# A decoder layer with an RWKV-7 branch: TensorE's order in the recurrence written out, and one chain step for two heads

## The chip, the cores and the metric

The kernel runs on one core of a Trainium2 chip. The metric is device time in microseconds (us) of one execution. The core has TensorE (PE, matrix products; PEld is its load of weights), VectorE (DVE), ScalarE (ACT), GpSimd (POOL) and SyncE (SP, which here issues every DMA). Each engine works through a queue of its own in order; semaphores tie the queues together.

## The reference

One layer over 1024 tokens of width 1024. After a norm, one product with `w_in` gives everything that the two branches of the mixer need. Branch A is a dilated window attention. Branch B is RWKV-7: for each of 16 heads of width 64 a state is carried through all tokens.

```
proj = h @ w_in[l]
S_t = S_{t-1} diag(w_t) + (S_{t-1} a_t) b_t^T + v_t k_t^T ;  y_t = S_t r_t
y  = (y - mean) * rsqrt(var + GN_EPS) * gn_w + gn_b + (sum(r*k*r_k)) * v
o_rwkv = y * (sigmoid(dg) @ g2)
merged = sigmoid(g_attn) * (o_attn @ wb[:256]) + sigmoid(g_rwkv) * (o_rwkv @ wb[256:])
x = x + gt1 * rms_norm(merged @ w_out)
x = x + gt2 * rms_norm(square(relu(norm(x) @ w_ff1)) @ w_ff2)
```

## The kernel before

Three stages follow one another: the start and the attention (to about 420 us of the span), the recurrence with branch B (to about 1364 us), then the merge, the output product and the feed-forward. Only the recurrence is touched by the change.

Channels go two heads at a time: a pair is 128 channels, one partition each, and there are eight pairs, m = 0 to 7. Time is cut into 16 chunks of 64 tokens. For each pair these steps follow one another; the letter is the one in the table `ORDER` (line 19).

- P, `pair_project`: three dense products with `w_in` (r, k, v). A dense job is 128 output channels by 1024 tokens: 8 blocks of k, each with a high and a low part of the float32 operands, 48 products of 128x512 in all (line 307). Its weights come by DMA in four pieces, are split by ACT (`w_h`) and POOL (`w_l`), and its result leaves one of two PSUM buffers `d` through ACT and DVE (`shifted`).
- E, `pair_lora`: small products for decay and rate, then tanh on ACT and a running sum on DVE. F, `pair_features`: the norm of k (`bones`, Ln, Exp), and the factors `ar` and `bk`.
- g, `pair_gram`: 32 small products, masked by DVE into `lm` and `fe`. V, `pair_values`. I, `pair_inverse`: a triangular inverse on DVE, 30 steps of two operations with a transpose before and behind (`lt`, lines 769 to 781).
- L, `pair_local`: `place` copies the inverse into block-diagonal tiles `bd`; three rounds of products (`s<-lt,bd`, line 838) give `eh`, and 32 products (`s<-fe,b`, line 853) the step matrices `fe`.
- C, `pair_chain`: the serial part. For each of 16 chunks and each of the two heads, one product of `fe` with the state `sv` (line 874); DVE scales the new state out of PSUM (line 877), and that is the operand of the head's next product.
- N, `pair_norm`: the norm of y, a transpose back, and the gate. G is one gate job: a dense job like those of P, whose result goes to DRAM for the merge. There are 16; the first runs ahead of the recurrence.

`ORDER` is the order in which the program issues these steps. It is not the order of the engines: a scheduler sorts the instructions by priority and by a cost model of its own, and puts dense products on TensorE where that model has TensorE waiting. Small products use two PSUM buffers `s`; those of E and of the norm of k use the buffers `d` of the dense jobs.

## Time and profile before

| | |
|---|---|
| median of 3 runs | 2263.57 us (2256.59 to 2266.53) |
| the profiled execution | 2252.45 us; its span, first to last instruction, 2250.7 us |
| TensorE busy | 2083.3 us (93% of the span), granted clock 0.968 of full |
| DVE, ACT, POOL busy | 1559.3, 1035.0, 602.6 us |
| recurrence, first to last product of the chains | 560.23 to 1310.86 us |

The granted clock is the share of 2.4 GHz that the chip gave TensorE; it has two levels, 1.2 and 2.4 GHz, so a mean of 0.968 is a mix. Busy shares over the whole span say little here, since the recurrence has other limits than the dense stages.

### The profile page before, as it was taken

What the parts mean: (1) busy time and instruction counts of PE and PEld (TensorE: products, weight loads), DVE (VectorE), ACT (ScalarE), POOL (GpSimd) and SP (SyncE); (2) the same over time, 40 slices, a digit from 0 to 9 for tenths busy, and PEclk for the clock granted to TensorE, in tenths of its full rate; (3) what the DMA queues carried; (4) which work ended last, traced back from release to release, by engine and by line L of the source; (5) the groups of instructions that cost most, each with busy time, mean ns of one, the idle gap of its engine ahead of it and who ended that gap; (6) DMA issues with size and microseconds to landing.
All of it is one profiled execution on the core that took longest, in us unless ns stands there. A gap on an engine that the chain in (4) does not pass through costs nothing. (4 is left out here: it accounts for less than half of the span.)

```text
span 2250.7 us, 28246 instructions
## 1 busy us (share of the span) xinstructions
PE 2083.3 (93%) x10002; PEld 1621.9 (72%) x10002; DVE 1559.3 (69%) x2857; ACT 1035.0 (46%) x2018; POOL 602.6 (27%) x455
## 2 busy tenths in 40 slices
PE   6899999988999989898989999999889999999997
PEld 2676766666777767676767778877667777788886
DVE  5845555458989787878777743436876553799988
ACT  4634533445454636454554442225744443533342
POOL 2504310321313131222122122201100000788850
PEclk9999999999999999999998999999999999999999
DMA  7513311110111110101011154432544333433232
GB/s 248 181 34 99 99 40 29 59 31 22 30 33 35 31 37 27 35 29 37 24 37 34 52 179 159 128 120 84 166 156 163 113 107 111 166 130 128 88 109 75
DMA packets 156315, 194.88 MB, mean 87 GB/s; under 512 B 10729, under 2 KB 110211, under 8 KB 154127
## 3 DMA queue, kind: packets, MB, share of 16 engines
q1 hardware_dynamic: 156175, 193.08, 25.8%
q8 instruction: 79, 1.29, 0.2%
q14 instruction: 61, 0.50, 0.1%
HBM read 152.14 MB, written 40.90 MB: 86 GB/s over the span
## 5 line engine op out<-in xcount | busy, mean ns | idle before, releaser
L307 PE MATMUL d<-hh,w_h 128*128 128x512 f32 x960 | 328.2, 414 | 8.0 <-ACT w_h L64 4.6
L307 PE MATMUL d<-hl,w_h 128*128 128x512 f32 x960 | 329.5, 413 | 2.9 <-DVE hl L280 2.9
L307 PE MATMUL d<-hh,w_l 128*128 128x512 f32 x960 | 324.2, 410 | 1.4 <-DVE w_l L65 1.3
L65 POOL TENSOR_TENSOR w_l<-w_t,w_h 128x256 fp32r<-128x256 f32 x160 | 128.3, 803 | 634.0 <-ACT w_h L64 288.7
L1108 PE MATMUL m<-op 128*128 128x512 f32 x1272 | 292.0, 391 | 6.3 <-DVE big L1344 2.4
L1108 PE MATMUL m<-big,op 128*128 128x512 f32 x1152 | 276.6, 401 | 8.0 <-ACT op L64 4.1
L1108 PEld LDWEIGHTS m<-op 128*128 128x128 f32 x1272 | 239.5, 189 | 58.5 <-POOL op L65 3.4
L1108 PEld LDWEIGHTS m<-big,op 128*128 128x128 f32 x1152 | 213.9, 189 | 70.8 <-DVE u L1219 5.3
L64 ACT CAST w_h<-w_t 128x256 fp32r<-128x256 f32 x272 | 108.4, 404 | 310.3 <-PE d L307 222.7
L307 PEld LDWEIGHTS d<-hh,w_h 128*128 128x128 f32 x960 | 180.4, 192 | 47.8 <-ACT w_h L64 5.8
L307 PEld LDWEIGHTS d<-hl,w_h 128*128 128x128 f32 x960 | 181.0, 192 | 44.9 <-issue 9.4
L307 PEld LDWEIGHTS d<-hh,w_l 128*128 128x128 f32 x960 | 180.1, 191 | 42.5 <-issue 7.9
L64 ACT CAST op<-t 128x512 fp32r<-128x512 f32 (+1 forms) x152 | 113.5, 775 | 174.5 <-PE m L1108 119.3
L153 POOL TENSOR_TENSOR macc<-macc,ada_t 128x512 f32<-128x512 f32 x56 | 87.2, 1559 | 179.5 <-ACT macc L151 160.7
L65 DVE TENSOR_TENSOR op<-t,op 128x512 fp32r<-128x512 f32 (+1 forms) x125 | 117.7, 962 | 20.5 <-ACT op L64 20.3
L1281 DVE TENSOR_TENSOR big<-big,m 128x1024 f32<-128x1024 f32 x88 | 104.7, 1210 | 11.9 <-PE m L1108 11.8
L1299 POOL TENSOR_TENSOR t<-big 128x1024 f32<-128x1024 f32 x7 | 23.1, 3303 | 325.8 <-DMA big<-in_w_ff_dram 325.4
L775 DVE TENSOR_TENSOR lt<-lt 64x30 f32<-64x30 f32 (+14 forms) x240 | 97.1, 404 | 8.2
L777 DVE TENSOR_TENSOR lt<-lt 64x30 f32<-64x30 f32 (+14 forms) x240 | 93.9, 391 | 7.7
L874 PEld LDWEIGHTS ch<-sv,fe 128*128 128x128 f32 x512 | 83.0, 190 | 20.2 <-DVE sv L877 8.9
L65 POOL TENSOR_TENSOR op<-t,op 128x1024 fp32r<-128x1024 f32 x27 | 88.4, 3275 | 7.1 <-ACT op L64 7.1
L65 DVE TENSOR_TENSOR w_l<-w_t,w_h 128x256 fp32r<-128x256 f32 x112 | 60.1, 545 | 40.3 <-ACT w_h L64 28.9
(381 smaller groups left out, 3888.4 us busy)
## 6 DMA issues: line engine op xcount, KB each, us to landing
w_t<-in_w_in_dram SPq DMA_DIRECT2D x240, 128.0 KB
ada_t<-in_ada_w_dram SPq DMA_DIRECT2D x64, 256.0 KB
fS<-ft SPq DMA_DIRECT2D x64, 256.0 KB
t<-in_w_ff_dram SPq DMA_DIRECT2D x16, 1024.0 KB
big<-fS SPq DMA_DIRECT2D x16, 1024.0 KB
big<-in_w_ff_dram SPq DMA_DIRECT2D x16, 1024.0 KB
x<-in_x_dram SPq DMA_DIRECT2D x16, 512.0 KB
ada_t<-in_ada_w_dram SPq DMA_DIRECT2D x16, 512.0 KB
```

The lines of the kernel that those rows point to most:

```text
L64: nc.scalar.copy(hi, t)
L65: (eng or nc.vector).tensor_tensor(lo, t, hi.bitcast(F32), OP.subtract)
L153: nc.gpsimd.tensor_tensor(acc, acc, t, OP.add)
L307: nc.tensor.matmul(p[:, 512 * half + cs.start:512 * half + cs.stop], a, b[half][k][:, cs], start=k == ks[0] and i == 0, stop=k == ks[-1] a ...
L775: nc.vector.tensor_tensor(q, lb[:, s + 1:32, s:s + 1].to_broadcast([64, n, s]), lb[:, s:s + 1, 0:s].to_broadcast([64, n, s]), OP.mult)
L777: nc.vector.tensor_tensor(lb[:, s + 1:32, 0:s], lb[:, s + 1:32, 0:s], q, OP.add)
L874: nc.tensor.matmul(ps[h][:, c8, :], fe[b][:, h, c8, :], sv[h][b][:, c8, :], start=True, stop=True)
L1108: self.nc.tensor.matmul(p, s, m, start=start and k == 0 and i == 0, stop=k == len(a) - 1 and i == 2, skip_group_check=not start)
L1281: nc.vector.tensor_tensor(acc[nm][h], acc[nm][h], ps2[h], OP.add)
L1299: vb.tensor_tensor(t3, wr[:, k2, h2], wr[:, k1, h2], OP.subtract)
```

## The change

`ORDER` goes. A method `recurrence` issues the steps; while `pinned` is set, TensorE's instructions keep exactly the order in which they are issued (`mm` and `tr`). From pair 1 on, the dense work (rows r, k, v of pairs 2 to 7 and gates 1 to 15, 33 jobs in all) is one stream, and `fill(us)` issues so much of it, in pieces of two products counted as 0.45 us. The amounts are the constants `FE` to `FN`. `fill_until` issues dense pieces until the v of the next pair is done. Gates 1 to 11 are spread over the pairs, and 12 to 15 come last; before, most gates stood behind the last chain.

The chain takes both heads in a step: two products into one PSUM tile, and one DVE operation that scales both states by a factor broadcast along 64 columns; `sv` holds both heads. E and the norm of k use PSUM buffers `s` in place of `d`. `pair_local` becomes `pair_moves` (up to the transposes) and `pair_solve`; `pair_norm` is cut into `pair_spread` and `pair_norm`. Tiles `lt` go from 3 to 6, and the weights of E get a buffer of their own.

```diff
-ORDER = "P0 E0 F0 g0 V0 I0 P1 L0 C0 E1 F1 N0 g1 I1 V1 L1 P2 G1 C1 E2 F2 N1 g2 I2 V2 L2 P3 G2 C2 E3 F3 N2 g3 I3 V3 L3 P4 G3 C3 E4 F4 N3 g4 I4 V4 L4 P5 G4 C4 E5 F5 N4 g5 I5 V5 L5 P6 G5 C5 E6 F6 N5 g6 I6 V6 L6 P7 G6 C6 E7 F7 N6 g7 I7 V7 L7 C7 N7 G7 G8 G9 G10 G11 G12 G13 G14 G15"
+LEAD, BETWEEN, LAST = (1, 2), ((3,), (4, 5), (6,), (7, 8), (9,), (10, 11)), (12, 13, 14, 15)
+FE, FF, FG, FI, FL, FM, FC, FN = 0.9, 6.0, 0.9, 22.0, 0.45, 0.45, 0.45, 9.0
...
-NBD, NFT, NLT, NW, NGT, NRK = 5, 6, 3, 4, 2, 4
+NBD, NFT, NLT, NW, NGT, NRK = 5, 6, 6, 4, 2, 4
...
+            self.recurrence(st, wp, psD, gS)
+    def recurrence(self, st, wp, psD, gS):
+        prs = {}
+        jobs = []
+        for j in LEAD:
+            jobs.append(("G", j))
+        for m in range(2, 8):
+            jobs += [(nm, m) for nm in "rkv"] + [("G", j) for j in BETWEEN[m - 2]]
+        jobs += [("G", j) for j in LAST]
+        self.fill_jobs, self.fill_done, self.fill_w, self.credit = jobs, set(), {}, 0.0
+        self.fill_at = self.fill_stream(st, wp, psD, gS, prs)
+        prs[0] = self.pair_project(st, 0)
+        self.pair_lora(st, prs[0], 0)
+        self.pair_norms(st, prs[0], 0)
+        self.pair_features(st, prs[0], 0)
+        self.pair_gram(st, prs[0], 0)
+        self.pair_values(st, prs[0], 0)
+        self.pair_inverse(st, prs[0], 0)
+        self.pair_moves(st, prs[0], 0)
+        prs[1] = self.pair_project(st, 1)
+        self.pair_solve(st, prs[0], 0)
+        self.pinned = True
+        for m in range(8):
+            pr, nx = prs[m], None
+            if m < 7:
+                if m:
+                    self.fill_until(("v", m + 1))
+                nx = prs[m + 1]
+                self.pair_lora(st, nx, m + 1)
+                self.fill(FE)
+                self.pair_norms(st, nx, m + 1)
+            self.pair_chain(st, pr, m)
+            if nx:
+                self.pair_features(st, nx, m + 1)
+                self.pair_spread(st, pr, m)
+                self.fill(FF)
+                self.pair_gram(st, nx, m + 1)
+                self.pair_inverse(st, nx, m + 1)
+                self.pair_values(st, nx, m + 1)
+                self.pair_norm(st, pr, m)
+                self.pair_moves(st, nx, m + 1)
+                self.fill(FI)
+                self.pair_solve(st, nx, m + 1)
+            else:
+                self.pair_spread(st, pr, m)
+                self.fill(FN)
+                self.pair_norm(st, pr, m)
+                self.fill_until(jobs[-1])
+        self.pinned = False
+    def mm(self, *a, **k):
+        i = self.nc.tensor.matmul(*a, **k)
+        return self.tc.keep_in_program_order(i) if self.pinned else i
+    def tr(self, *a, **k):
+        i = self.nc.tensor.transpose(*a, **k)
+        return self.tc.keep_in_program_order(i) if self.pinned else i
+    def fill_weights(self, wp, n):
+        if n < len(self.fill_jobs):
+            nm, i = self.fill_jobs[n]
+            c0 = C_GATE + 128 * i if nm == "G" else C_RWKV + 1024 * "rkv".index(nm) + 128 * i
+            self.fill_w[n] = self.load_w(wp, self.w("w_in")[:, c0:c0 + 128], "w", 2, NW, 2, self.nc.gpsimd)
+    def fill_stream(self, st, wp, psD, gS, prs):
+        self.fill_weights(wp, 0)
+        for n, (nm, i) in enumerate(self.fill_jobs):
+            self.fill_weights(wp, n + 1)
+            w = self.fill_w.pop(n)
+            p = psD.tile([128, S], F32, name="d")
+            for k in range(KT):
+                wh, wl = w[k]
+                for e, (x, b) in enumerate(((wh, self.hh2), (wh, self.hl2), (wl, self.hh2))):
+                    for half in range(2):
+                        self.mm(p[:, 512 * half:512 * half + 512], x, b[half][k], start=k == 0 and e == 0,
+                                stop=k == KT - 1 and e == 2)
+                    if k == KT - 1 and e == 2:
+                        if nm == "G":
+                            self.gate_out(wp, gS, p, i)
+                        else:
+                            t = st["f4"].tile([128, S], F32, name="rkv", bufs=NRK)
+                            self.shifted(p, t, 8 * "rkv".index(nm) + i)
+                            prs.setdefault(i, {})[nm] = t
+                        self.fill_done.add((nm, i))
+                    yield
+    def fill(self, us):
+        if not self.pinned:
+            return
+        self.credit += us
+        while self.credit >= 0.45:
+            self.credit -= 0.45
+            next(self.fill_at, None)
+    def fill_until(self, job):
+        while job not in self.fill_done:
+            next(self.fill_at)
 
...
-        pw, pa = [st["psD"].tile([128, S], F32, name="d") for i in range(2)]
         for hs in halves:
-            p = pw[:, hs]
-            nc.tensor.matmul(p, lh[:, 0, :], st["dws"][:, hs], start=True, stop=False)
-            nc.tensor.matmul(p, ll[0:64], st["dws"][0:64, hs], start=False, stop=True)
+            p = st["psS"].tile([128, 512], F32, name="s")
+            self.mm(p, lh[:, 0, :], st["dws"][:, hs], start=True, stop=False)
+            self.mm(p, ll[0:64], st["dws"][0:64, hs], start=False, stop=True)
...
+    def pair_norms(self, st, pr, m):
+
+        nc = self.nc
+        k, C = pr["k"], lambda nm: self.c(nm, m)
+        halves = [slice(0, 512), slice(512, 1024)]
+        ch = lambda ap: ap.rearrange("p (c t) -> p c t", t=64)
+        pr["bk"] = bk = st["b8"].tile([128, 16, 2, 64], F32, name="b8")
+        for i, hs in enumerate(halves):
+            n = bk[:, 8 * i:8 * i + 8, 1, :]
+            nc.scalar.activation(n, ch(k[:, hs]), AF.Square, scale=C("k_k"))
+            p = st["psS"].tile([128, 512], F32, name="s")
+            self.mm(ch(p), self.bones, n, start=True, stop=True)
+            nc.vector.tensor_scalar(n, ch(p), 1e-24, None, op0=OP.max)
+        for i in range(2):
+            n = bk[:, 8 * i:8 * i + 8, 1, :]
+            nc.scalar.activation(n, n, AF.Ln, scale=float(2 ** 20))
...
-        sv = [[f4.tile([128, 8, 64], F32, name="sv", bufs=6) for b in range(2)] for h in range(2)]
-        pr.update(ar=ar, bk=bk, dd=dd, sv=sv)
+        sv = [f4.tile([128, 2, 8, 64], F32, name="sv", bufs=3) for b in range(2)]
...
-            for h in range(2):
-                for e in range(2):
-                    nc.scalar.copy(sv[h][i][0:64, e:8:2, :], pv[64 * e:64 * e + 64, :, 64 * h:64 * h + 64])
+            for e in range(2):
+                nc.scalar.copy(sv[i][0:64, :, e:8:2, :],
+                               pv[64 * e:64 * e + 64].rearrange("p q (h t) -> p h q t", h=2))
...
+            self.fill(FG)
...
-    def pair_local(self, st, pr, m):
+    def pair_moves(self, st, pr, m):
...
+        pr.update(place=place, bds=bds, xx=xx)
+
+    def pair_solve(self, st, pr, m):
...
+                self.fill(FL)
...
+                self.fill(FM)
...
-        for h in range(2):
-            nc.gpsimd.memset(sv[h][0][64:128, 0, :], 0.0)
-        for b in range(2):
-            ps = [st["psC"].tile([128, 8, 64], F32, name=f"ch{h}") for h in range(2)]
-            for c8 in range(8):
-                c = 8 * b + c8
+        nc.gpsimd.memset(sv[0][64:128, :, 0, :], 0.0)
+        for q in range(4):
+            ps = st["psC"].tile([128, 4, 2, 64], F32, name=f"ch{q % 2}")
+            for i in range(4):
+                c = 4 * q + i
                 for h in range(2):
-                    nc.tensor.matmul(ps[h][:, c8, :], fe[b][:, h, c8, :], sv[h][b][:, c8, :],
+                    self.mm(ps[:, i, h, :], fe[c // 8][:, h, c % 8, :], sv[c // 8][:, h, c % 8, :],
                                      start=True, stop=True)
-                    if c < 15:
-                        nc.vector.tensor_scalar(sv[h][(c + 1) // 8][64:128, (c + 1) % 8, :], ps[h][64:128, c8, :],
-                                                dd[64:128, h, c:c + 1], None, op0=OP.mult)
+                if c < 15:
+                    nc.vector.tensor_tensor(sv[(c + 1) // 8][64:128, :, (c + 1) % 8, :], ps[64:128, i],
+                                            dd[64:128, :, c:c + 1].to_broadcast([64, 2, 64]), OP.mult)
+                self.fill(FC)
             for h in range(2):
-                nc.scalar.copy(y[64 * h:64 * h + 64, 8 * b:8 * b + 8, :], ps[h][0:64])
+                nc.scalar.copy(y[64 * h:64 * h + 64, 4 * q:4 * q + 4, :], ps[0:64, :, h, :])
         pr["y"] = y
 
-    def pair_norm(self, st, pr, m):
+    def pair_spread(self, st, pr, m):
...
+    def pair_norm(self, st, pr, m):
...
```

The order on each engine, as built, at the places that matter below. First TensorE where pair 3's products of `fe` end and its chain begins, before (`s<-fe` are the step matrices, `lora` and `bones` belong to the next pair, `ch` is the chain, `d<-h` dense):

```order
L853 MATMUL s<-fe,b_6817 128x128 x4
L853 MATMUL s<-fe,b_6820 128x128 x4
L645 MATMUL d<-dws,lorah 128x512
L646 MATMUL d<-dws,loral 128x512
L853 MATMUL s<-fe,b_6817 128x128 x4
L874 MATMUL ch_7255<-sv,fe 128x64
L652 MATMUL d<-das,lorah 128x512
L653 MATMUL d<-das,loral 128x512
L683 MATMUL d<-b_7360,bones 128x512
L853 MATMUL s<-fe,b_6820 128x128 x4
...
L307 MATMUL d<-hh,w_h 128x512 x2
L874 MATMUL ch_7256<-sv,fe 128x64
```

And now, one pair later (the rows between the first two and the lora rows are dense pieces):

```order
L643 MATMUL s<-fe,b_7178 128x128 x4
L643 MATMUL d<-hh,w_l 128x512 x2
...
L643 MATMUL s<-das,lorah 128x512
L643 MATMUL s<-das,loral 128x512
L643 MATMUL d<-hh,w_h 128x512 x2
L643 MATMUL d<-hl,w_h 128x512 x2
L643 MATMUL s<-b_7451,bones 128x512 x2
L643 MATMUL ch_7464<-sv,fe 128x64 x2
L643 MATMUL d<-hh,w_l 128x512 x2
L643 MATMUL ch_7464<-sv,fe 128x64 x2
L643 MATMUL d<-hh,w_h 128x512 x2
```

The chain no longer starts among the products of `fe`; it stands behind all of them and behind the next pair's lora and bones, and each of its steps has one dense piece.

TensorE from the last gram to the wait for the inverse, before (`T` are products with `ident`, `dgs` is the gate of the norm):

```order
L785 MATMUL s<-ident,b_8234 128x128 x8
L307 MATMUL d<-hh,w_h 128x512 x2
L722 MATMUL s<-center,rkv 128x128 x4
L729 MATMUL s<-rkv,brk 128x512
L307 MATMUL d<-hl,w_h 128x512 x2
L307 MATMUL d<-hh,w_l 128x512
L722 MATMUL s<-center,rkv 128x128 x4
L729 MATMUL s<-rkv,brk 128x512
L307 MATMUL d<-hh,w_l 128x512
```

And now:

```order
L647 MATMUL s<-ident,b_7451 128x128 x16
L643 MATMUL s<-center,rkv 128x128 x4
L643 MATMUL s<-rkv,brk 128x512
L643 MATMUL s<-center,rkv 128x128 x4
L643 MATMUL s<-rkv,brk 128x512
L647 MATMUL ch_7864<-ident,lt 128x128 x4
L647 MATMUL ch_7873<-ident,lt 128x128 x4
L643 MATMUL ch_7883<-dgs,g_6488 128x512
L643 MATMUL ch_7886<-dgs,g_6488 128x512
L647 MATMUL s<-ident,b_7670 128x128 x8
L647 MATMUL s<-ident,ar 128x128 x4
```

The dense rows that stood between the small products are gone from here; 96 or 98 dense products follow in one block behind it.

TensorE at the last pair's norm, before:

```order
L900 MATMUL ch_10534<-ident,lt 128x128 x4
L900 MATMUL ch_10543<-ident,lt 128x128 x4
L307 MATMUL d<-hh,w_l 128x512 x2
...
L911 MATMUL ch_10556<-dgs,g_9950 128x512
L307 MATMUL d<-hl,w_h 128x512
L307 MATMUL d<-hh,w_l 128x512 x2
...
L307 MATMUL d<-oh_11296,wbr_h 128x512 x2
```

And now:

```order
L647 MATMUL ch_11125<-ident,lt 128x128 x4
L647 MATMUL ch_11134<-ident,lt 128x128 x4
L643 MATMUL ch_11144<-dgs,g_10082 128x512
L643 MATMUL ch_11147<-dgs,g_10082 128x512
L309 MATMUL d<-oh_11176,wbr_h 128x512 x2
```

`oh` is the merge's operand, loaded from DRAM. Before, dense gate jobs fill TensorE between the last chain and the merge; now nothing dense stands behind the last norm.

## Rows read from the trace of the kernel before

**Rows 1.** Windows: length, busy (count) of PE PEld DVE ACT POOL, clock, DMA share, GB/s

```profile
560.23:1310.86 750.63, 682.46 (x3714) 545.52 (x3713) 606.07 (x1363) 377.75 (x785) 170.11 (x203) 0.94 0.11 34
1310.86:1364.09 53.23, 50.92 (x223) 40.67 (x222) 20.47 (x27) 27.13 (x45) 17.33 (x16) 1.00 0.69 225
1364.09:1500.00 135.91, 134.37 (x592) 110.67 (x591) 58.03 (x62) 35.11 (x56) 33.31 (x20) 1.00 0.46 146
```

**Rows 2.** Timeline of PE: first chain product of pairs 0-3 and 7, the last

```profile
560.23 0.33 PE L874 MATMUL ch<-sv,fe 128*128 128x64 f32 x2
...
659.45 0.33 PE L874 MATMUL ch<-sv,fe 128*128 128x64 f32 x2
...
757.42 0.55 PE L874 MATMUL ch<-sv,fe 128*128 128x64 f32 x4
...
867.89 0.33 PE L874 MATMUL ch<-sv,fe 128*128 128x64 f32 x2
...
1291.35 0.33 PE L874 MATMUL ch<-sv,fe 128*128 128x64 f32 x2
...
1310.53 0.33 PE L874 MATMUL ch<-sv,fe 128*128 128x64 f32 x2
```

**Rows 3.** Timeline of DVE: first transpose into, first out of, two inverses

```profile
698.32 2.01 DVE L769 STREAM_TRANSPOSE lt<-b 32x1024 f32<-32x1024 f32 x1
...
731.85 1.89 DVE L781 STREAM_TRANSPOSE lt<-lt 32x1024 f32<-32x1024 f32 x1
...
808.36 1.96 DVE L769 STREAM_TRANSPOSE lt<-b 32x1024 f32<-32x1024 f32 x1
...
842.51 1.89 DVE L781 STREAM_TRANSPOSE lt<-lt 32x1024 f32<-32x1024 f32 x1
```

**Rows 4.** Windows of PE alone: length, busy (count), clock, DMA share, GB/s

```profile
708.00:712.00 4.00, 2.92 (x15) 1.00 0.33 131
...
796.00:800.00 4.00, 3.65 (x12) 0.50 0.00 0
...
848.00:852.00 4.00, 4.00 (x18) 0.50 0.12 36
```

**Rows 5.** Groups by line, 540 to 1330 us: busy, mean ns, idle before, releasers

```profile
L877 DVE TENSOR_SCALAR sv<-ch,dd 64x64 f32<-64x64 f32 x240 | 63.4, 290 | 23.0 <-PE ch L874 19.7
...
L845 DVE COPY b<-s 32x512 f32<-32x512 f32 x64 | 43.8, 685 | 2.8 <-ACT lt L843 1.9
L845 ACT COPY b<-s 32x512 f32<-32x512 f32 x64 | 37.0, 578 | 13.9 <-PE s L838 13.2
...
L904 ACT ACTIVATE lt<-ch,col 64x256 f32<-64x256 f32 x64 | 35.9, 561 | 15.9 <-PE ch L900 15.0
...
L855 DVE TENSOR_TENSOR fe<-s,ar 64x256 f32<-64x256 f32 x64 | 27.3, 427 | 48.1 <-ACT fe L854 47.4
...
L787 ACT COPY fe<-s 128x256 f32<-128x256 f32 x56 | 17.3, 382 | 2.6 <-PE s L785 2.2
...
L805 ACT COPY bd<-b 32x128 f32<-32x128 f32 x56 | 16.6, 297 | 36.4 <-DVE b L755 35.7
...
L655 ACT ACTIVATE ft<-d,half 128x512 f32<-128x512 f32 x14 | 9.6, 683 | 2.5 <-PE d L653 2.4
```

**Rows 6.** Timeline of PE: four chain records that waited; the product behind an idle stretch

```profile
770.80 0.66 PE L874 MATMUL ch<-sv,fe 128*128 128x64 f32 x4
...
846.86 1.97 PE L816 MATMUL s<-ident,b 128*128 128x128 f32 x8 [5.25 <-ACT lt L817]
```

**Rows 7.** Timeline: last pair's output stored; operands `oh` of the merge loaded and cast

```profile
1328.81 0.34 SPq L913 DMA_DIRECT2D oS<-lt  x1
...
1334.89 0.50 SPq L927 DMA_DIRECT2D gr<-oS  x1
...
1339.31 1.05 ACT L64 CAST oh<-gr 128x1024 fp32r<-128x1024 f32 x1 [0.84 <-DMA gr<-oS]
...
1362.29 1.05 ACT L64 CAST oh<-gr 128x1024 fp32r<-128x1024 f32 x1 [3.91 <-DMA gr<-oS]
```

More of the change, by code (lines that the diff above doesn't have):

```diff
@@ L597, in rwkv @@
-            for word in ORDER.split():
-                if word[0] != "G" or int(word[1:]) >= NGA:
-                    step[word[0]](int(word[1:]))
+            self.recurrence(st, wp, psD, gS)
[46 more added lines that the diff above has]
+                self.fill_until(jobs[-1])
+        self.pinned = False
@@ L623, in pair_lora @@
         cm = slice(128 * m, 128 * m + 128)
-        lw = wp.tile([128, 2, 128], F32, name="w_t", bufs=2)
+        lw = wp.tile([128, 2, 128], F32, name="lw", bufs=1)
         lh = wp.tile([128, 2, 128], F32R, name="lorah", bufs=1)
@@ L676, in pair_features @@
         cft = lambda ap: ap.rearrange("p c (f t) -> p f c t", f=2)
-        pn = st["psD"].tile([128, S], F32, name="d")
-        for i, hs in enumerate(halves):
-            n = bk[:, 8 * i:8 * i + 8, 1, :]
-            nc.scalar.activation(n, ch(k[:, hs]), AF.Square, scale=C("k_k"))
-            p = pn[:, hs]
-            nc.tensor.matmul(ch(p), self.bones, n, start=True, stop=True)
-            nc.vector.tensor_scalar(n, ch(p), 1e-24, None, op0=OP.max)
-        for i in range(2):
-            n = bk[:, 8 * i:8 * i + 8, 1, :]
-            nc.scalar.activation(n, n, AF.Ln, scale=float(2 ** 20))
         for i, hs in enumerate(halves):
@@ L784, in pair_inverse @@
             for c in range(4):
-                nc.tensor.transpose(p[:, c, :], bk[:, 4 * b + c].rearrange("p a t -> p (a t)"), self.ident)
+                self.tr(p[:, c, :], bk[:, 4 * b + c].rearrange("p a t -> p (a t)"), self.ident)
             for h in range(2):
@@ L819, in pair_local @@
             for g in range(4):
-                nc.tensor.transpose(p[:, g, :], ar[:, 0, 512 * f + 128 * g:512 * f + 128 * g + 128], ident)
+                self.tr(p[:, g, :], ar[:, 0, 512 * f + 128 * g:512 * f + 128 * g + 128], ident)
             for h in range(2):
                 nc.scalar.copy(xx[h][:, f, :, 64:128], p[:, :, 64 * h:64 * h + 64])
+        pr.update(place=place, bds=bds, xx=xx)
+    def pair_solve(self, st, pr, m):
+        nc = self.nc
+        b8, psS = st["b8"], st["psS"]
+        ident, ar4, fe, place, bds, xx = self.ident, pr["ar4"], pr["fe"], pr["place"], pr["bds"], pr["xx"]
+        ehs = []
         for h in range(2):
@@ L837, in pair_local @@
                 for g in range(4):
-                    nc.tensor.matmul(p[:, g, :], bds[h][i][:, g, :], x[i // 2][:, g, :], start=True, stop=True)
+                    self.mm(p[:, g, :], bds[h][i][:, g, :], x[i // 2][:, g, :], start=True, stop=True)
                 if i == 1:
@@ L852, in pair_local @@
                 for c in range(4):
[L853 removed]
+                    self.mm(p[:, c, :], ehs[h][:, 4 * b + c, :], fb[:, c, :], start=True, stop=True)
                 nc.scalar.copy(fb[0:64], p[0:64])
@@ L899, in pair_norm @@
                 cc = 8 * b + 2 * c
-                nc.tensor.transpose(p[:, c, :], y[:, cc:cc + 2, :].rearrange("p a b -> p (a b)"), self.ident)
+                self.tr(p[:, c, :], y[:, cc:cc + 2, :].rearrange("p a b -> p (a b)"), self.ident)
             for h in range(2):
```

41 lines of the change are left out of this document (17 added, 24 removed).

## The prediction

> **What bounds the kernel now.** The windows come first, to see which stages the change can touch [rows 1]. In the recurrence TensorE is busy 682.46 of 750.63 us at a mean clock of 0.94. That mean is a mix of 2.4 and 1.2 GHz with 12% of the time at the lower level. As work done there takes twice its time, at most 0.06 x 750.63 = 45 us is lost to the clock, and 68.2 us to idling. In the 53.2 us behind the last chain TensorE is busy 50.92 us at clock 1.00: the gate jobs cover the last norm and the loads of the merge. Later stages are not touched. The merge's first window gives the price of dense work at full clock: 134.37 us / 592 = 0.227 us a product, 0.453 us a piece of two, 10.9 us a job of 48.
>
> Next the timeline of the chains, which gives the period of the loop over pairs [rows 2]: seven periods take 1291.35 - 560.23 = 731.1 us, 104.4 us each. Inside a period there is one dependent path: chain, features, gram, inverse, solve, next chain. The timeline of DVE cuts it into three [rows 3]. From a chain's start to the inverse's start there are 38.9 us (659.45 to 698.32) or 50.9 us (757.42 to 808.36). The inverse takes 37.3 us, up to the end of its second transpose out, 731.85 + 2 x 1.89 = 735.6 (in the other pair 38 us, to 846.3). From there to the next chain there are 21.8 and 21.6 us. TensorE is about 91% busy beside this path, so path and TensorE are near each other, and the change is judged by both: dense work doesn't vanish, it only moves.
>
> Third, windows of 4 us on TensorE show what its clock did [rows 4]; fourth, the groups by line give the durations and releasers [rows 5]; last, single records of the chain and of the tail [rows 6, 7].
>
> **The change part by part**, for one period.
>
> *Lora and bones, now ahead of the chain.* Four tiles go through two `s` buffers, paced by ACT's tanh of 0.683 us [rows 5]: 4 x 0.683 = 2.7 us. With the two bones products, 4 x 0.227 us of dense pieces and the first wait for ACT I take 5.5 us (bounds: 2.7, ACT alone; 8, if no two tiles overlap). Before, they lay beside the chain. Now the chain waits for them.
>
> *Chain.* Before, DVE had two operations a step of 0.290 us [rows 5], and a product of the chain came out 0.66 us after its release where it had waited [rows 6]. Now DVE has 15 operations on 64x128, which the trace doesn't show. The nearest rows are 0.290 for 64 columns and 0.427 for 256 (L855), so they bound it; I take 0.33. A step is 0.66 + 0.33 + about 0.06 between engines = 1.05 us. TensorE's own work in it, two chain products and one piece, is 0.45 + 0.453 = 0.91 us: it waits 0.14 us a step. The last chain, alone, takes 16 x 1.05 = 16.8 us where it took 19.5 (1291.35 to 1310.86): -2.7 us.
>
> The Trainium skill ("VectorE: DVE Perf Modes", section "The TRN2 errata — SBUF-src ops pay a fixed extra latency per instruction") gives an operation from PSUM 120 cycles and one for each column at 0.96 GHz: 0.192 us for 64 columns, where the trace has 0.290. By its slope alone 64 more columns would make it 0.357 us, which would add 15 x 0.03 = 0.4 us a chain, some 3 us in all. It changes no step above.
>
> *Chain's start to the inverse's start.* DVE is saved 30 x 0.290 - 15 x 0.33 = 3.7 us, so 35.2 us from the short case, 47.2 from the long one. I take the short one, since the chain no longer shares its start with `fe` products.
>
> *Inverse against TensorE.* On DVE the inverse stays 37.3 us and meets about 0.6 us of evictions: 37.9. TensorE in the same time has all its small products (transposes of bk, values, norm, moves) with nothing dense between, then 98 dense products. The small ones leave through ACT: 8 x 0.382 + 8 x 0.297 + 8 x 0.561 [rows 5] + 12 copies of the kind of the first, about 4.6: 14.5 us, some 17.3 with values and the gaps between two buffers (bounds 14.5 and 20). The block is 98 x 0.227 = 22.2 us. 17.3 + 22.2 = 39.5: TensorE is the later by 1.6 us.
>
> *Solve.* Before, the next chain began 21.7 us behind the inverse, among the `fe` products. Now it begins behind all of them. The copies into `eh` on DVE are 8 x 0.685 = 5.5 us [rows 5], and ACT's 8 x 0.578 = 4.6; with three rounds of products and two adds I take 13.4 us to the last, then eight tiles. A tile's four products take 0.49 us at full clock (eight took 1.97 at half [rows 6]), ACT's copy about 0.38, DVE's two adds 2 x 0.427: 1.7 us around one buffer, plus some 0.3 between engines. With two buffers that is 1.0 us a tile if they overlap in full, 2.0 if not; I take 1.5, 8 x 1.5 = 12. Together 25.5 us (bounds 21.5 and 29.5).
>
> Period: 5.5 + 35.2 + 39.5 + 25.5 = 105.7 us, against 104.4.
>
> *`fill_until`.* In three pairs the products that the pieces have not yet issued are 36, 24 and 22, which stand in one block ahead of the lora: 82 x 0.227 = 18.6 us, with nothing of the path beside them.
>
> From the first to the last chain's start: 7 x 105.7 + 18.6 - 5.5 (the first lora lies ahead of it) = 753.0 against 731.1: +21.9. The first chain starts later too, behind all `fe` products of pair 0, the lora and the bones: +8 (bounds 0 and 14). The last chain ends at +21.9 + 8 - 2.7 = +27.2 us.
>
> *The tail.* Before, 53.2 us lie between the last chain and the merge, all dense. Now 42 dense products, 9.5 us, stand in it, all ahead of the norm's end, and the merge waits for its operands. Before, the last pair's output was stored 18 us behind the chain, the next load took 4.4 us up to its cast, and the last cast of `oh` came just before the merge [rows 7]. The merge's loads that share one buffer follow each other: 4.4 + 1.05 for the cast + about 1.2 for the rest of the split = 6.6 us, four of them behind the 18 us plus 1.5: last operand at 46 us. By then the merge has done those parts of its first two columns that it has operands for, 10 of 20 blocks: 60 x 0.227 = 13.6 us. So it is as if the merge began at 46 - 13.6 = 32.4 us: -20.9 us (bounds: -27 and -8, if it begins in effect 26 or 45 us behind the chain).
>
> *Clock.* At 708 to 712 us TensorE was busy 2.92 of 4 us with its clock at 1.00; at 796 to 800 and at 848 to 852 it was 0.50, the latter behind an idle stretch of 5.25 us [rows 4, 6]. The small products without dense ones are sparser than before. If the clock falls in them, the block behind starts at half rate and loses about 2 us a pair; I take a third of that, +5 us (bounds 0 and 14).
>
> The Trainium skill ("TensorE: Matmul & The Clock Gate", section "A second HAM failure mode: psum-queue depth-cycling") says that idling between small groups which wait for evictions can make the clock swing. That speaks against this change. The window at 708 us shows no such fall; by the rule the sum would be 9 us longer, by the row 5 us shorter.
>
> Sum: +27.2 - 20.9 + 5 = +11.3 us on the profiled 2252.45, so 2263.7. The profiled execution is 11.1 us under the median of the runs shown, 2263.57; against that the forecast is 2274 us after rounding down by 0.9.
>
> **The rivals.**
>
> *B, faster.* TensorE always has the next piece, idles nowhere over 2.5 us, and the lower clock is gone; the small products' stretch is covered by DVE's 37.9 us (gaps nearer the lower bound, 14.5 + 22.2 = 36.7), and solve takes 22.5. Period 5.5 + 35.2 + 37.9 + 22.5 = 101.1. 7 x (101.1 - 105.7) = -32 us, and the clock term goes: 2274 - 37 = 2237. For it: up to 45 us lie in the clock, and 68 us of idling. Against: the rows show the path as long as TensorE's work, so one of the two must give.
>
> *C, slower.* TensorE's strict order turns DVE's queue into a stall. L855 waited 47.4 us for ACT, and L805 35.7 for DVE [rows 5]: such operations queue in front of a chain's operation, and TensorE, which before took other dense pieces, now stands at the chain's next product with one piece done. It decides once this holds DVE by more than 5 us a pair; chain to inverse then comes to 40 us in place of 35.2 (still under the 47 of the long case), the period to 110.5: 7 x 4.8 = +34 us, 2308 us.
>
> *D, nothing comes of it.* Dense pieces take the place of idling that the scheduler had already filled as well; period 104, the tail gives back what `fill_until` costs: 2264 us.
>
> **How the numbers follow.** A measurement of this kernel tells about 0.5%, 11 us, from no change. The likeliest case, periods of 104 to 109, has 0.47 and its own range of 2258 to 2290; half of it is within 0.5%, half slower. B has 0.29 (0.27 faster, 0.02 same), C 0.19 (slower), D 0.05 (same). Faster 0.27; same 0.235 + 0.02 + 0.05 = 0.305; slower 0.235 + 0.19 = 0.425. The range reaches somewhat past the centres of B and C, to 2233 and 2312, so that about 0.11 and 0.08 are left out.
>
> **What would show it right or wrong.** The first chain products of the pairs, 105 to 106 us apart, right; near 101, B; near 110, C. Chain products in twos, one DVE operation of 0.33 us behind them, steps of 1.05 us. ACT, not DVE, named as releaser of TensorE in the small products behind the inverse's start, and TensorE reaching the first solve product about when the inverse ends. 32 to 46 us from the last chain to the merge, with TensorE idle there behind the norm. A granted clock in the recurrence above 0.94 but not 1.00. The forecast fails if the clock goes to 1.00 and TensorE's idling doesn't grow, or if DVE's chain operation waits for anything but TensorE.

## The result, and the profile after

The changed kernel takes 2296.0 us (median of 4 runs, 2283.72 to 2300.14), before 2262.17 (4 runs): a ratio of 1.0142, 95% interval 1.0094 to 1.019. It is slower by 1.4%. The profiled execution spans 2298.4 us, 47.7 more than before; that is more than the 33.8 between the medians, since the execution profiled before was faster than the median, and the one after slower.

Windows of TensorE from the end of the attention to the merge's last product, before and then after; columns as in [rows 4].

```profile
420.00:1472.90 1052.90, 968.24 (x5000) 0.95 0.17 55
```

```profile
420.00:1518.70 1098.70, 979.25 (x4994) 0.95 0.16 52
```

45.8 of the 47.7 us arise in here. The products are the same (a few records are missing), so length less busy time is TensorE's idling: 84.7 us before, 119.5 after. That is +34.8 us; the other +11.0 are busy time of the same products. The mean clock, to two digits, is the same. Between the first and the last chain product it has even risen, from 0.94 [rows 1] to 0.96:

```profile
573.05:1379.10 806.05, 719.40 (x3860) 0.96 0.12 37
```

At most 0.04 x 806 = 32 us are lost to the clock there, before 45, so the lower clock is not what made the recurrence longer. Its busy time is up by 37 us, since dense products that stood behind the last chain now stand in it (3860 products, before 3714); TensorE's idling there is 86.7 us, before 68.2.

The timeline of TensorE's chains in after, which answers to [rows 2]:

```profile
573.05 0.56 PE L643 MATMUL ch<-sv,fe 128*128 128x64 f32 x4
...
690.56 0.55 PE L643 MATMUL ch<-sv,fe 128*128 128x64 f32 x4
...
802.01 0.55 PE L643 MATMUL ch<-sv,fe 128*128 128x64 f32 x4
...
918.74 0.55 PE L643 MATMUL ch<-sv,fe 128*128 128x64 f32 x4
...
1362.32 0.55 PE L643 MATMUL ch<-sv,fe 128*128 128x64 f32 x4
...
1378.44 0.66 PE L643 MATMUL ch<-sv,fe 128*128 128x64 f32 x4
```

Seven periods take 789.3 us, 112.8 each, where they took 104.4; they alternate between 116 to 118 (with a block of `fill_until`) and 111 to 113, and the one without lora has 102.3. The last chain takes 16.8 us to its end, it took 19.5.

In the mean of the seven pairs, the way from a chain's start to the inverse's start fell from 44.8 to 36.0 us. From there to the first product of the solve it is 41.6, before 41.0. But from that product to the next chain's start it grew from 18.7 to 35.1 us: the chain now stands behind all `fe` products, `fill_until`, lora and bones. That is 16.4 us a pair lost against 8.7 won.

One period in detail, the pair whose chain starts at 802.01. DVE, the inverse's ends (answers to [rows 3]):

```profile
837.46 3.91 DVE L868 STREAM_TRANSPOSE lt<-b 32x1024 f32<-32x1024 f32 x2
...
869.37 4.21 DVE L880 STREAM_TRANSPOSE lt<-lt 32x1024 f32<-32x1024 f32 x2
```

And TensorE in the same period, the places between which the time passes:

```profile
848.61 1.23 PE L643 MATMUL ch<-dgs,g 128*128 128x512 f32 x2 [2.00 <-ACT lt L1019]
850.92 2.08 PE L643 MATMUL ch<-dgs,g 128*128 128x512 f32 x2 [1.09 <-ACT lt L1019]
...
857.28 0.71 PE L643 MATMUL d<-hh,w_h 128*128 128x512 f32 x2
...
879.64 0.61 PE L643 MATMUL s<-lt,bd 128*128 128x128 f32 x4
...
903.93 1.05 PE L643 MATMUL s<-fe,b 128*128 128x128 f32 x8
...
910.76 0.40 PE L643 MATMUL s<-dws,lorah 128*128 128x512 f32 x1
...
916.28 2.62 PE L643 MATMUL s<-b,bones 128*128 128x512 f32 x4
918.74 0.55 PE L643 MATMUL ch<-sv,fe 128*128 128x64 f32 x4
```

The inverse ends at 873.58. TensorE has waited for ACT among its small products until 857.28, then works through its block of dense pieces, and comes to the solve at 879.64, 6.1 us late. `fill_until` stands from 905.3 to 910.76; lora and bones take 8.0 us to the chain, with the clock at 0.79 in the mean (bones take 2.62 us for four records, in the pair before 1.88 at 1.00). The windows of this stretch, in the pair before and in this one:

```profile
795.48:802.01 6.53, 6.17 (x17) 1.00 0.07 20
910.76:918.74 7.98, 7.71 (x18) 0.79 0.07 20
```

Whom TensorE waited for in the recurrence (waiter, releaser, us in total, times, longest), first in after, then in before:

```profile
PE s L643 <- DVE b L952: 23.7, 13, 4.0
PE ch L643 <- ACT lt L1019: 20.7, 14, 2.0
PE ch L643 <- DVE sv L985: 12.7, 29, 0.8
PE s L643 <- ACT b L952: 10.0, 14, 1.2
PE s L647 <- ACT fe L886: 8.1, 14, 0.8
```

```profile
PE s L816 <- ACT lt L817: 30.7, 7, 5.2
PE s L749 <- DVE fe L757: 7.5, 3, 2.5
PE s L729 <- DVE rkv L730: 7.3, 4, 3.1
PE s L853 <- ACT b L845: 4.8, 7, 1.2
```

Before, nearly half of it is one place, the wait for the inverse, 4.4 us a pair. There TensorE stands at the transposes, released by a copy on ACT (L817) that is queued behind the inverse. After, that place is gone, and five kinds of short waits have come, each of a small product that stands next in the order: for copies into `eh` (L952, on DVE and on ACT), the norm's eviction (L1019), the chain's DVE operation (L985), the copies of the transposes (L886).

In the tail the merge's first product stands 17.0 us behind the last chain (53.2 before), and it then waits for operands. After, on SP and ACT (answers to [rows 7]):

```profile
1398.83 0.32 SPq L1028 DMA_DIRECT2D oS<-lt  x1
1399.93 0.32 SPq L1042 DMA_DIRECT2D gr<-oS  x1
...
1422.74 1.05 ACT L66 CAST oh<-gr 128x1024 fp32r<-128x1024 f32 x1 [5.45 <-DMA gr<-oS]
```

The last pair's output leaves 20 us behind the chain, the last operand is cast 45 us behind it. To the merge's last product it is 139.6 us from the last chain, before 162.0.

### The profile page after: what moved, and what is told of

Its sections match the earlier page's. It is cut to its first block, busy times and chain, and to the rows that moved or that the text cites. A ratio compares the mean times of both kernels' runs of the same rounds, so it can differ in the third digit from the quotient of the medians.

```text
span 2298.4 us, 28089 instructions
## 1 busy us (share of the span) xinstructions
PE 2094.0 (91%) x10002; PEld 1592.6 (69%) x10002; DVE 1544.0 (67%) x2737; ACT 1041.2 (45%) x2018; POOL 597.5 (26%) x447
## 5 line engine op out<-in xcount | busy, mean ns | idle before, releaser
L643 PE MATMUL d<-hh,w_h 128*128 128x512 f32 x528 | 175.4, 414 | 0.0
L643 PE MATMUL d<-hl,w_h 128*128 128x512 f32 x528 | 174.6, 412 | 0.0
L643 PE MATMUL d<-hh,w_l 128*128 128x512 f32 x528 | 172.6, 408 | 0.0
L309 PE MATMUL d<-hh,w_h 128*128 128x512 f32 x432 | 141.8, 405 | 4.0 <-ACT w_h L66 4.0
L309 PE MATMUL d<-hh,w_l 128*128 128x512 f32 x432 | 141.7, 404 | 3.8 <-DVE w_l L67 3.8
L309 PE MATMUL d<-hl,w_h 128*128 128x512 f32 x432 | 142.5, 405 | 1.9 <-DVE hl L282 1.9
L67 DVE TENSOR_TENSOR op<-t,op 128x512 fp32r<-128x512 f32 (+1 forms) x125 | 117.6, 963 | 20.5 <-ACT op L66 20.3
L643 PEld LDWEIGHTS ch<-sv,fe 128*128 128x128 f32 x512 | 70.0, 195 | 58.1 <-DVE sv L985 41.2
L874 DVE TENSOR_TENSOR lt<-lt 64x30 f32<-64x30 f32 (+14 forms) x240 | 102.5, 427 | 7.6
L643 PEld LDWEIGHTS d<-hh,w_h 128*128 128x128 f32 x528 | 94.4, 193 | 16.8 <-issue 2.0
L643 PEld LDWEIGHTS d<-hl,w_h 128*128 128x128 f32 x528 | 94.6, 193 | 16.2
L643 PEld LDWEIGHTS d<-hh,w_l 128*128 128x128 f32 x528 | 93.1, 190 | 15.0
```

Of the source, the lines that this page charges most:

```text
L67: (eng or nc.vector).tensor_tensor(lo, t, hi.bitcast(F32), OP.subtract)
L309: nc.tensor.matmul(p[:, 512 * half + cs.start:512 * half + cs.stop], a, b[half][k][:, cs], start=k == ks[0] and i == 0, stop=k == ks[-1] a ...
L643: i = self.nc.tensor.matmul(*a, **k)
L874: nc.vector.tensor_tensor(q, lb[:, s + 1:32, s:s + 1].to_broadcast([64, n, s]), lb[:, s:s + 1, 0:s].to_broadcast([64, n, s]), OP.mult)
```

## The experiments

Ratios are against the kernel before, with 95% intervals. The changed kernel stands at 1.0142 [1.0094, 1.019].

**1. Dense pieces between the small products.** `FX` is 0.45; the call stands behind each of 18 groups in transposes, values, norm and moves.

```diff
-FE, FF, FG, FI, FL, FM, FC, FN = 0.9, 6.0, 0.9, 22.0, 0.45, 0.45, 0.45, 9.0
+FE, FF, FG, FI, FL, FM, FC, FN = 0.9, 6.0, 0.9, 22.0 - 18 * 0.45, 0.45, 0.45, 0.45, 9.0
...
+            self.fill(FX)
```

> 18 of the 49 dense pieces that stood in one block ahead of the solve (FI) are put between the small products behind the inverse's start: after each group of transposes, values, norm and moves. The amount of dense work per pair is the same. Theory 1 (TensorE is late for the solve, by 4.6 us in the mean, since its small products wait for ACT with nothing dense between and in part at half clock): the pieces fill idle time, the block shrinks by 8.1 us, TensorE reaches the first solve product within 1.5 us of the inverse's end, periods fall by 3 to 4 us, total -25 us against the changed kernel, some 2271 us. Theory 2 (the sum of TensorE's work decides wherever it stands): the stretch grows by what the block loses, the solve starts when it did, 0 +- 8 us.

Ratio 1.0129 [1.0095, 1.0163]: no gain that can be told. The mechanism of theory 1 is there, its gain in time is not. TensorE comes to the solve 0.6 to 2.3 us behind the inverse, and the way from the inverse's start to the solve falls from 41.6 to 38.2 us in the mean, 24 us in all. Some 16 of them come back: the solve grows from 25.9 to 27.2 us, the way from the chain's start to the inverse's start by 0.6, lora by 0.5. Windows of one pair's small products and of its solve, after and then this kernel (third number from the end is the clock):

```profile
727.33:747.79 20.46, 15.23 (x73) 0.83 0.08 30
769.89:795.17 25.28, 20.26 (x140) 1.00 0.07 21
```

```profile
729.88:753.41 23.53, 19.48 (x107) 1.00 0.08 25
767.79:796.57 28.78, 22.79 (x140) 0.88 0.08 22
```

In this pair the low clock has moved from the small products, where pieces now fill the gaps, to the solve, where the changed kernel kept 1.00. In all seven pairs the small products now have 1.00. Five solves are below it, where one was, and so are five of six stretches of lora and bones, where three were. The clock from the first to the last chain is 0.96 in both kernels.

**2. v finished later.**

```diff
-                    self.fill_until(("v", m + 1))
+                    self.fill_until(("k", m + 1))
...
+                if m:
+                    self.fill_until(("v", m + 1))
                 self.pair_values(st, nx, m + 1)
```

> The dense pieces that finish the next pair's v are no longer issued in one block ahead of the lora; only k must be done there, and v just ahead of the values (where the pieces of chain and features have long issued it). Theory 1 (these 82 products, 20.5 us over three pairs in the trace, lie alone on the path, and the same work behind the last chain is hidden under the merge's loads): the three long periods fall from 116.8 to 111.5 us, the tail holds 90 products in place of 42, total -12 to -20 us, some 2280 us. Theory 2 (the work only moves, and the merge starts later by what it adds): 0 +- 8 us.

Ratio 1.0175 [1.0142, 1.0209]. The periods do lose 12 us (777.4 in all), but k still had to be waited for twice, and the merge's first product comes 30.3 us behind the last chain. To the merge's last product 5.8 us are left of the 12, and the total shows nothing (spans 2297.7 and 2298.4 us). The total is theory 2's, the shorter periods are theory 1's in part.

**3. Lora and bones in the chain.** `side` yields behind each tile.

```diff
-                self.pair_lora(st, nx, m + 1)
-                self.fill(FE)
-                self.pair_norms(st, nx, m + 1)
-            self.pair_chain(st, pr, m)
+            self.pair_chain(st, pr, m, self.side(st, nx, m + 1) if nx else None)
...
                 self.fill(FC)
+                if side:
+                    next(side, None)
```

> The next pair's lora and bones go into the chain: four lora tiles behind its first four steps, two bones products behind steps 5 and 6; the two pieces FE between them go. Theory 1 (they take 7.3 us ahead of each chain in six pairs, with TensorE waiting for ACT's tanh and for the bones operand): the chain grows by some 2 us, since TensorE has only 0.14 us to spare in a step, the period falls by 5, total -30 us, some 2266 us. Theory 2 (DVE's scans of 1.23 us and ACT's work then stand in the chain's way, one step each): the chain grows by 5 us or more, total -10 us or less of a gain.

Ratio 1.03 [1.0273, 1.0328], clearly slower; both theories fell. The chain grew by only 2.6 us (theory 1 was near), yet from the chain's start to the inverse's start it is 44.9 us, 36.0 before the edit. What follows the chain is not released by it but by the features, and these begin with bones and Ln. ACT's Ln in after, in the pair from 802.01, and here, in the pair from 692.68:

```profile
802.82 1.15 ACT L766 ACTIVATE b<-b 128x512 f32<-128x512 f32 x2
```

```profile
703.31 0.63 ACT L770 ACTIVATE b<-b 128x512 f32<-128x512 f32 x1
```

0.8 us behind the chain's start there, 10.6 here. So lora, bones, features is the path, and the chain lies beside it: taking lora out of the way of the chain did not help.

**4. All three edits.** 

> The three edits together: dense pieces between the small products, v finished ahead of the values, lora and bones in the chain. Theory 1 (three separate losses on one path): the gains add up, -60 to -75 us against the changed kernel, 2221 to 2236 us, less than the kernel before. Theory 2 (TensorE's total work bounds): about 2285 us or more; theory 3 (the path on DVE and ACT takes over once TensorE is no longer late): half the sum, some 2260 us.

Ratio 1.0202 [1.0182, 1.0222], 2305.77 us: theories 1 and 3 fell. The time is one that theory 2 allows (2285 us or more), but its reason is not seen: TensorE idles 136.9 us from 420 us to the merge's last product, 17 more than without the edits, so it isn't its work that bounds.

**5. The two-head chain alone, in the kernel before.**

```diff
-                for h in range(2):
-                    nc.tensor.matmul(ps[h][:, c8, :], fe[b][:, h, c8, :], sv[h][b][:, c8, :],
...
+                if c < 15:
+                    nc.vector.tensor_tensor(sv[(c + 1) // 8][64:128, :, (c + 1) % 8, :], ps[64:128, i],
+                                            dd[64:128, :, c:c + 1].to_broadcast([64, 2, 64]), OP.mult)
```

> The kernel before with one part of the change: the chain takes both heads in a step (one state tile, one DVE operation of 64x128). Order, buffers and gates are those of before. Theory A (the loss of the change lies in the written-out order, and the two-head step is worth what it saves): the last chain falls from 19.2 to 16 us and the chain's start to the inverse's start by about 2 to 4 us in each pair, total -10 to -25 us against before, some 2245 us. Theory B (the step for two heads loses the freedom to let the heads drift apart): the chain grows beside dense work, +5 to +20 us.

Ratio 1.008 [1.0055, 1.0105]: theory B's sign and size (12.8 us between the medians). But its reason is hardly seen: the first seven chains take 27.2 us in the mean, before 28.5; only the last grows, from 19.5 to 20.4. The same window as above shows idling of 92.0 us (+7.3) and more busy time (+24) at a lower clock:

```profile
420.00:1504.40 1084.40, 992.37 (x5007) 0.93 0.17 53
```

**6. The changed kernel, order left to the scheduler.**

```diff
-        return self.tc.keep_in_program_order(i) if self.pinned else i
+        return i
```

> The changed kernel with the same program and amounts of dense work, but TensorE's order left to the scheduler (nothing is pinned). Theory A (the pinned order is the cost: lora and bones wait behind all fe products, the chain behind both): lora goes back among the fe products and the chain starts there too, 10 us less between solve and chain in a pair, and the gates move behind the last chain; total 2245 to 2270 us. Theory B (the program's own structure is the cost: the amounts, two s buffers for lora as well): within 10 us of the changed kernel's 2296.

2247.19 us in these rounds, ratio 0.9961 [0.992, 1.0001]: theory A's time, and the one edit that undoes the loss. The window:

```profile
420.00:1466.50 1046.50, 955.51 (x5000) 0.95 0.18 55
```

Idling is 91.0 us, 28.5 less than pinned, busy time 23.7 less. The order on TensorE, from the timeline around one chain's start:

```profile
885.48 0.62 PE L643 MATMUL d<-hh,w_l 128*128 128x512 f32 x2
885.95 0.40 PE L643 MATMUL s<-dws,lorah 128*128 128x512 f32 x1
...
888.57 0.40 PE L643 MATMUL s<-dws,lorah 128*128 128x512 f32 x1
888.89 0.50 PE L643 MATMUL s<-dws,loral 64*128 64x512 f32 x1
889.32 0.43 PE L643 MATMUL ch<-sv,fe 128*128 128x64 f32 x2
889.56 0.48 PE L643 MATMUL s<-das,lorah 128*128 128x512 f32 x1
889.98 0.49 PE L643 MATMUL s<-das,loral 64*128 64x512 f32 x1
890.40 0.43 PE L643 MATMUL ch<-sv,fe 128*128 128x64 f32 x2
```

Lora, chain and dense pieces are mixed, and differently in each pair: periods run from 96 to 119 us. From the first product of the solve to the next chain's start it is 23.0 us in the mean, 12 less than pinned, as theory A had it; from a chain's start to the inverse's start 44.7, as before the change. The gates did not move behind the last chain: the merge's first product stands 20.9 us behind it, and the merge's last product 140.8. So against the kernel before, seven periods are 14 us longer in all and the tail is 21 us shorter.

**7. Lora and bones in the solve**, still pinned, through the PSUM buffers of the chain.

```diff
-                self.pair_solve(st, nx, m + 1)
+                self.pair_solve(st, nx, m + 1, self.side(st, prs.setdefault(m + 2, {}), m + 2) if m < 6 else None)
...
                 self.fill(FM)
+                if side:
+                    next(side, None)
```

> The changed kernel with the next pair's lora and bones issued among the products of fe in the solve (through the chain's idle PSUM buffers, so that they don't compete for s); chain, features and amounts as they are. Theory A (the path between chains runs lora, bones, features, gram; lora in the chain only made it longer, but TensorE, ACT and DVE have idle time in the solve): the 7.3 us ahead of the chain go, the solve grows by 2 to 3 us, total -20 to -30 us, some 2270 us. Theory B (the solve is as full as the chain was: ACT's tanh and DVE's scans delay the fe tiles by as much): 0 +- 10 us.

Ratio 1.0187 [1.0139, 1.0234], theory B. The 7.3 us are gone (44 in all), but the solve takes 3.7 us more (+26), chain's start to inverse's start 1.8 more (+13), and `fill_until` 4.5 in all, since two pieces a pair are no longer issued.

**8. Experiments 1, 2 and 7 together.** 

> The changed kernel with the dense pieces between the small products, v finished only ahead of the values, and lora and bones among the products of fe. Theory A (the three stretches are separate, and each gives what it gave alone, the clock's half rate included): -4 -2 -25 = some 2262 us, the same as before. Theory B (with TensorE's gaps closed, the clock stays up and the gains that the clock took from the spread pieces return): 2235 to 2250 us. Theory C (TensorE's work bounds the period once the gaps are closed): no better than the lora edit alone, 2270 or more.

Ratio 1.0176 [1.0139, 1.0213], 2300.58 us: theories A and B fell, and the time is one that C allows (2270 or more). C's reason is not seen: its solve takes 36.2 us in the mean, and TensorE idles 131.8 us, so the gaps were not closed.

**9. A chain for each head again, pinned.**

```diff
...
-                    nc.vector.tensor_tensor(sv[(c + 1) // 8][64:128, :, (c + 1) % 8, :], ps[64:128, i],
-                                            dd[64:128, :, c:c + 1].to_broadcast([64, 2, 64]), OP.mult)
...
+                        nc.vector.tensor_scalar(sv[(c + 1) // 8][64:128, h, (c + 1) % 8, :], ps[h][64:128, c8, :],
+                                                dd[64:128, h, c:c + 1], None, op0=OP.mult)
```

> The changed kernel, its order pinned as it is, with one edit undone: the chain has one PSUM tile and one DVE operation of 64x64 for each head again. Theory A (one operation for both heads saves DVE 0.29 us a step, and in a pinned order nothing can use the freedom of two heads): steps of 1.05 us grow to about 1.3, the last chain from 16.1 to about 19.5 us, the chain's start to the inverse's start by 2 to 4 us, +15 to +30 us against the changed kernel, 2311 to 2326. Theory B (with two heads apart, TensorE's piece and the other head's product lie beside each DVE operation, and the step doesn't grow): -5 to +5 us.

Ratio 1.0215 [1.0185, 1.0245], 7 us above the changed kernel's median, between the theories, and the intervals touch. The last chain is not longer but a little shorter, 15.6 us to its end against 16.8. So theory A's reason is wrong for the lone chain: what shortened the last chain against before (19.5) was the written order with one dense piece for each step, not the joint operation. Where the order is the scheduler's, the joint step makes the last chain longer too, 20.4 against 19.5 in the kernel before (experiment 5) and 21.2 against 20.3 in the changed one (experiments 6 and 10). The cost lies beside the features: chain's start to inverse's start is 37.6 us against 36.0.

**10. A chain for each head, order free.** 

> The changed kernel with TensorE's order left to the scheduler, and with one tile and one DVE operation for each head in the chain again. Theory A (as with the two-head step put alone into the kernel before, which cost 13 us there: TensorE's clock and idling suffer from a step that waits for both heads): 10 to 15 us less than with the scheduler's order and the two-head step, 2232 to 2240 us. Theory B (the two-head step saves DVE work on the path here): 5 to 20 us more, 2252 to 2267 us.

Ratio 1.0065 [1.0042, 1.0087], theory B, 20 us above experiment 12 on the same chip (2271.87 against 2252.19). Put into the old program the two-head step costs (experiment 5), in the new program, with the order free, it pays. What decides that is open.

**11. v finished later, order free.** 

> The changed kernel with TensorE's order left to the scheduler, and v asked for only ahead of the values. Theory A (with the order free, a block of dense pieces ahead of the lora is only a place in the program; the scheduler puts it into gaps anyway): within 6 us of the scheduler's order alone, 2247. Theory B (the block still lies on the path in the long periods): -10 to -20 us, some 2232 us.

Ratio 1.0008 [0.9986, 1.003], 2257.65 us: no gain, so theory B fell. It is 5 us above experiment 12, which ran beside it, and so within theory A's bound of 6; it is 10 above the 2247 that theory A names.

**12. Experiment 6 again, five rounds.** 

> The changed kernel with TensorE's order left to the scheduler once more, in five rounds, since its first interval against the kernel before touched 1. Theory A (it is faster than before: idling and chain as in its first trace): ratio 0.993 to 0.997 with an interval under 1. Theory B (no difference): ratio 0.998 to 1.002.

Ratio 0.9988 [0.9968, 1.0008]: theory B. With the order free, the rest of the change makes no difference that these runs can tell. No version is faster than the kernel before by more than its interval.

Idling and busy time of TensorE from 420 us to the merge's last product, in us, one trace each:

| order by the scheduler | idle, busy | order pinned | idle, busy |
|---|---|---|---|
| before | 84.7, 968 | changed | 119.5, 979 |
| two-head chain alone | 92.0, 992 | pieces spread | 117.8, 977 |
| changed, order free | 91.0, 956 | v later | 121.1, 972 |
| the same again | 89.6, 962 | lora in the chain | 145.2, 978 |
| free, chain by heads | 88.1, 986 | three edits | 136.9, 965 |
| free, v later | 83.1, 974 | lora in the solve | 130.4, 972 |
| | | 1, 2 and 7 | 131.8, 973 |
| | | chain by heads | 125.5, 976 |

Idling separates the pinned orders from the free ones. Among the free ones it does not follow the time: the chain by heads idles less than the changed kernel with its order free and takes some 20 us more, which lie in busy time.

## Why the prediction was right, and where it was wrong

Slower was forecast, with 2274 us and a likeliest range of 2258 to 2290; 2296 lies 6 us above that, inside the whole range. The sign and the path were right, the size was not: between the medians the change is 33.8 us, where some 10 were forecast. That 2296 still lies inside the range is owed to its width, since it reaches past the centres of both B and C. One of its own signs spoke against it as well: chains 105 to 106 us apart were to show it right, near 110 C, and they stand 111 to 113 apart where no block of `fill_until` stands between. The steps, in us:

| step | forecast | measured |
|---|---|---|
| lora and bones ahead of the chain | 5.5 | 7.3 (6.4 to 8.2) |
| chain's start to inverse's start | 35.2 | 36.0 |
| inverse's start to the solve | 39.5 | 41.6 |
| solve | 25.5 | 25.9 |
| `fill_until`, three pairs | 18.6 | 19.6 |
| first to last chain's start | 753.0 | 789.3 |
| first chain's start | +8 | +12.8 |
| last chain | -2.7 | -2.7 |
| end of the last chain | +27.2 | +68.2 |
| tail | -20.9 | -22.4 |

- **The path** was the right one, and the tail's working held: last operand at 46 us forecast, 45 measured, and a merge that begins in effect 30.8 us behind the chain (53.2 less 22.4) where 32.4 was forecast. That the merge's loads queue behind the last norm was read rightly from [rows 7]. The last chain's 16.8 us came as forecast, but experiment 9 shows that the joint operation is not what shortened it.
- **Mis-sized: "TensorE is the later by 1.6 us".** It was 4.6 us late in the mean. The small products took 19.6 us in place of 17.3, and the norm's evictions stood on the path (20.7 us of waits for L1019). The way from the inverse's start to the solve, 41.6 us in place of 39.5, makes 15 us of the 36 that the forecast of the periods lacks.
- **Mis-sized: lora and bones.** 7.3 us against 5.5, 10.6 us in all; 6.4 to 6.5 where the clock stayed up, 8.0 and more where it fell. The working paced the tiles by ACT's tanh. But TensorE itself is busy 6.17 of 6.53 us in the stretch before 802.01, at clock 1.00: its own products are the step. The solve (whose 13.4 and 12 make 25.4, not the 25.5 of the working) and the features give the rest, 2.7 and 5.7 us, `fill_until` and the gaps around it 2.
- **Mis-sized: the clock.** It was given 5 us, as a third of some 2 us a pair. But the clock fell in the small products of nearly every pair: 0.83 in five, 0.91 in one, 1.00 in one. Windows of the small products in the pair from 802.01 and in the next one:

```profile
837.46:857.53 20.07, 15.13 (x73) 0.83 0.08 30
954.50:972.47 17.97, 12.61 (x73) 1.00 0.02 5
```

  At 1.00 they take 18.0 us, near the 17.3 of the working, in the five pairs at 0.83 they take 20.2. So some 2 us are what a fall went with, and taking a third of them was the mistake. The place was another too, since the block behind kept 1.00 in all seven pairs. The single window at 708 us, [rows 4], on which I discounted the fall, did not stand for the new order. The Trainium skill ("TensorE: Matmul & The Clock Gate", section "A second HAM failure mode: psum-queue depth-cycling") reports of a bf16 kernel that short idling of TensorE between groups of products, as it cycles through PSUM banks, makes the clock swing; this trace agrees, with TensorE busy 15.13 of 20.07 us at 0.83. That TensorE waits for evictions there is read from this trace (L1019, L886), not from the page. The clock does not explain the loss against the kernel before, though, since over the recurrence it rose from 0.94 to 0.96. What made the 11 us of added busy time is not shown.
- **The DVE rule.** The Trainium skill ("VectorE: DVE Perf Modes", section "The TRN2 errata — SBUF-src ops pay a fixed extra latency per instruction") gives one cycle for each column at 0.96 GHz, by which 64 more columns would cost an estimated 67 ns. The new operation on 64x128 took 0.295 us, the old one, of another form, on 64x64 0.290 [rows 5]: no such step is seen between the two, and the 0.33 taken was too much.

```profile
L985 DVE TENSOR_TENSOR sv<-ch,dd 64x128 f32<-64x128 f32 x120 | 35.4, 295 | 32.2 <-PE ch L643 29.0
```

- **Rival C** named a time, 2308, nearer than mine, but not what happened: TensorE did wait for the chain's DVE operation, which had stood behind operations of the features and the norm of k in DVE's queue (29 waits, 12.7 us). Yet the inverse began nearly as forecast, 36.0 us behind the chain's start and not 40, since the features set it (experiment 3).
- **What the working missed** is that its terms are not independent. Experiments 1, 3 and 7 each closed the gap that they aimed at, and the time came back elsewhere. A sum over TensorE shows in the trace after what single gaps do not: the same work, one wait of 4.4 us a pair gone, and five kinds of new ones come. That the pinned order is the cause is shown by experiments 6 and 12, which change nothing else. Which of its pins matter, and whether some other written order does as well as the scheduler's, stays open.

## What to carry to other kernels

When an engine near its limit gets a fixed order, count its idling over the whole stage, length less busy time, and do not go by single gaps alone: work moved into one gap can leave another. A fixed order seems safe only where what it waits for comes at the same time in every round, which these runs suggest and do not test; here the eight kernels with a pinned order idled 118 to 145 us, the six with the scheduler's 83 to 92. Before moving a step off the path, ask what releases the work behind it: here the features, not the chain.

## What the runs showed of the hardware

- A DVE product out of PSUM with a factor broadcast along 64 columns took 0.295 us for 64x128, against 0.290 for a plain scaling of 64x64: twice the data, in another form of the operation, at nearly the same price.
- In one pair, dense pieces among the small products raised the clock there from 0.83 to 1.00, and in the next stretch, the solve, it was 0.88 in place of 1.00. Over the recurrence it was 0.96 with and without the pieces.
- At clock 1.00 the lora products of 128x512 stood 0.43 us apart on TensorE, the dense ones of the same size 0.23. Why is not shown.

```profile
798.42 0.50 PE L643 MATMUL s<-das,lorah 128*128 128x512 f32 x1
798.85 0.49 PE L643 MATMUL s<-das,loral 64*128 64x512 f32 x1
799.27 0.72 PE L643 MATMUL d<-hh,w_h 128*128 128x512 f32 x2
799.83 0.63 PE L643 MATMUL d<-hl,w_h 128*128 128x512 f32 x2
800.30 1.88 PE L643 MATMUL s<-b,bones 128*128 128x512 f32 x4
```
